# Three kinds of values turned by VectorE and DRAM instead of TensorE in a four-branch hybrid backbone

## The chip, the cores and the metric

One core of a Trainium2 chip runs the whole kernel in one launch. The metric is the device time of one execution in microseconds (us), the median of several.

## What is computed

Two layers of a backbone over 128 context tokens and 512 latent tokens (`T = 640` together), model width 1024, everything in float32. In each layer a modulated RMS norm gives `h`; one projection `h @ w_in` feeds four mixers of width 512: retention, a gated linear recurrence, a gated DeltaNet and HGRN2. Three of them have four heads of width 128 and run in both directions. Their outputs are gated, projected, summed and added to the residual. Cut to the values, the `v` below, which are what the change is about:

```python
(aq, ak, av, az, bx, bz, cq, ck, cv, cz, ca, cb, dq, df, di, dz, mg) = jnp.split(h @ w_in, offs, axis=-1)
# retention: values av.  kv = sum_j k_j k_dec_j v_j ; o = (q k^T * decay) v + q_dec (q state)
o_intra = jnp.einsum('bnhij,bnjhe->bnihe', scores, v)
kv = jnp.einsum('bnjhd,jh,bnjhe->bnhde', k, k_dec, v)
# DeltaNet: values are silu(conv(cv)); scaled by beta, then a triangular solve
rhs_v = jnp.moveaxis(v * beta[..., None], 3, 2)
# HGRN2: values di, used as in retention with a decay of its own for each channel
kv = jnp.einsum('bnjhd,bnjhe->bnhde', k * jnp.exp(bc[:, :, -1:] - bc), v)
```

## The kernel before

`layer_jobs` makes a list of jobs. A job is one weight tile of 128 columns: `load_w` (L332) loads 512 KB on SyncE's (SP's) queue, `split_w` copies it to a high part on ScalarE (`whi`, L359) and subtracts on VectorE for the low part (`wlo`, L361), and `product` (L376) multiplies in three passes (high by high, high by low, low by high) over eight pieces of 128 rows, first for tokens 0 to 383, then for 384 to 639: 48 matmuls a tile. The result lies channel by token, 128 x 640, and is evacuated from PSUM (`pj`, two banks) by a function `ev_*`. Raw tiles, high parts and low parts have two buffers each.

Beside the jobs run the mixers, Python generators in two lanes, G (DeltaNet heads) and HRL (HGRN2, retention and recurrence heads, alternating). After each piece of `product` the function `pace` advances the generator whose time has come by a count of TensorE time (`clock`, the numbers in `yield`). Each lane has one PSUM tile of two banks for wide results (`M2`, L171 and after). A scheduler then sets the final order on each engine; engines and queues run in that order.

A mixer that sums over tokens needs its values token by channel. `transposes` (five 128 x 128 transposes on TensorE, L301, into an `M2` tile) turns them:

- retention: `ret_in` projects `ak`, `aq`, then `av`, evacuated by `ev_copy` on ScalarE (L496). `ret_mix` waits for `av`, transposes it, copies it to `rvt` on ScalarE (L1298), yields 1.5, and goes on with the transposes of the keys. `rvt` is first read by the state matmuls (`m<-rvt,rkt`).
- HGRN2: `hgrn_in` projects `dq`, two `df`, then `di` (L496); `hgrn_mix` waits for `di`, transposes it and copies it to `hvt` (L1136). `hvt` is first read after seven levels of score work.
- DeltaNet: `gdn_prep` convolves `cv` into `vs`, transposes that, and one VectorE instruction (L939) scales it by 0.5 and the key norms `ik` into `vt`, read in `gdn_chain`.

The products of `rest` (modulation of later parts, `mod_dots`, L630, 64 loads and 128 VectorE dot products `mjunk`) run as fill beside the first heads of layer 0. `finish` stores a head's result to DRAM on SP's queue (`br<-fbr`, L565). `gdn_solve` and `gdn_inv` already move blocks of 32 through DRAM (`l_dr`, `d_dr`, loads `dct`, L992), and one VectorE transpose in blocks of 32 stands in L998.

Of the kernel before, what the change touches and what calls it, by code (L numbers as in the profile page):

```python
# [23 lines left out]
F32 = mybir.dt.float32  # L24
F32R = mybir.dt.float32r
U8 = mybir.dt.uint8
AF = mybir.ActivationFunctionType
# [47 lines left out]
def conv_off(t):  # L75
    return 0 if t == 0 else SC + 3 + 128 * (t - 1)
# [3 lines left out]
def hybrid_kernel(ctx: ExitStack, tc: tile.TileContext, I, O):  # L80
# [81 lines left out]
    def t3(ap, n=NT):  # L162
        return ap.rearrange("p (t c) -> p t c", t=n)

    def ts(t):
        return slice(128 * t, 128 * t + 128)
# [355 lines left out]
        return f  # L522


    def transposes(src_of, n=NT):
        ps = M2()
        for t in range(n):
            tr(ps[:, ts(t)], src_of(t), ident)
        return ps
# [244 lines left out]
    def layer(l, hh, hl):  # L774
# [6 lines left out]
        def proj_to(S, key, name, i, evac, shape=None, after=None):  # L781
# [5 lines left out]
                S[key] = x  # L787
            return Job(I['w_in'][l, CIDX[name, i]], run, cost=2 if name == 'df' else 1)

        def zproj(name, i, S):  # L790
            extra_jobs.append(proj_to(S, 'z', name, i, ev_silu2))
            zout[lane[0] - 1] = 1
            extra_jobs[-1].urgent = True
# [77 lines left out]
        def gdn_prep(h, S):  # L871

            yield lambda: 'ck' in S
            cs = gdn_conv(h, S, 'ck')
            yield LV
            ps = transposes(lambda t: cs[:, conv_off(t):conv_off(t) + 128])  # L880
            ss = sum_squares(t3(ps))
            S['kt'] = U(name="kt")
            A.activation(S['kt'], ps, AF.Copy)
            V.tensor_scalar(ss, ss, 4 * EPS, None, op0=OP.add)
            rk, ik = small_tile([128, NT], "rk", 1), small_tile([128, NT], "ik", 1)
            power(ik, ss, phalf)
            V.reciprocal(rk, ss)
            b2, kd = small_tile([128, 2, NT], "b2", 1), small_tile([128, 2, NT], "kd", 1)
            for d in range(2):
                c = 4 * d + h  # L890
                V.tensor_tensor(b2[:, d], rk, gg['beta'][:, :, c], op=OP.mult)
                V.tensor_tensor(kd[:, d], b2[:, d], gg['kd'][:, :, c], op=OP.mult)
            S['b2'], S['kd'] = b2, kd
            yield 2
            gms = []
            for d in range(2):
                R = gc_rows(d, h)
                msk = K('add_f') if d == 0 else K('add_b')
                V.tensor_tensor(t3(R), t3(R), msk[:, None, :].to_broadcast([128, NT, 128]), op=OP.add)
                for t in range(NT):  # L900
                    A.activation(R[:, ts(t)], R[:, ts(t)], AF.Exp, bias=gg['gcn'][:, t, 4 * d + h:4 * d + h + 1])
                gms.append(R)
            kc = S['kn'] = cs

            def tk(t):
                return kc[:, conv_off(t):conv_off(t) + 128]
            ps = M2()
            for t in range(NT):
                mm(ps[:, ts(t)], tk(t), tk(t), start=True, stop=True)
            for d in range(2):  # L910
                at = U(name="at")
                for t in range(NT):
                    V.scalar_tensor_tensor(at[:, ts(t)], ps[:, ts(t)], b2[:, d, t:t + 1],
                                           gms[d][:, ts(t)], op0=OP.mult, op1=OP.mult)
                S['at', d] = at
            yield gdn_solve(h, S)
            yield 2
            yield lambda: 'cq' in S
            qs = S['qn'] = gdn_conv(h, S, 'cq')
            yield LV  # L920
            sq = U([128, PADW], name="sq")
            A.activation(sq[:, :CONVW], qs[:, :CONVW], AF.Square)
            ps = column_sums(lambda t: sq[:, conv_off(t):conv_off(t) + 128])
            S['eps'] = small_tile([128, NT], "ssq", 1)
            V.tensor_scalar(S['eps'], ps, EPS * 128, 4 * EPS * EPS * 128, op0=OP.mult, op1=OP.add)
            yield 2
            ps = M2()
            for t in range(NT):
                mm(ps[:, ts(t)], tk(t), qs[:, conv_off(t):conv_off(t) + 128], start=True, stop=True)
            for d in range(2):  # L930
                V.tensor_tensor(gms[d], ps, gms[d], op=OP.mult)
                S['attn', d] = gms[d]
            yield 1.5
            yield lambda: 'cv' in S
            vs = gdn_conv(h, S, 'cv')
            yield LV
            ps = transposes(lambda t: vs[:, conv_off(t):conv_off(t) + 128])
            S['vt'] = U(name="vt")
            V.scalar_tensor_tensor(t3(S['vt']), t3(ps), 0.5, ik[:, :, None].to_broadcast([128, NT, 128]),  # L939
                                   op0=OP.mult, op1=OP.mult)  # L940
            yield 1

        def gdn_solve(h, S):
# [99 lines left out]

        def gdn_chain(h, S):
            kn, kt, vt = S['kn'], S['kt'], S['vt']
            SH, VN, QE = {}, {}, {}
            for d in range(2):
                SH[d] = U(name="gS")
# [63 lines left out]
        def hgrn_in(h, S):  # L1112
            def gates(d):
                def after(th):
                    c = 8 * l + 4 * d + h
                    k = S['k', d] = UP(name="hk%d" % d)
                    V.tensor_scalar(k, th, hbn[:, c:c + 1], hb[:, c:c + 1], op0=OP.mult, op1=OP.add)
                    V.tensor_scalar(th, th, hb[:, c:c + 1], ha[:, c:c + 1], op0=OP.mult, op1=OP.add)
                    V.tensor_scalar(th, th, 1e-30, None, op0=OP.max)
                return after  # L1120
            return [proj_to(S, 'q', 'dq', h, ev_silu2)] + \
                [proj_to(S, ('f', d), 'df', 4 * d + h, ev_tanh, after=gates(d)) for d in range(2)] + \
                [proj_to(S, 'v', 'di', h, ev_copy)]

        def hgrn_mix(h, S):
            yield lambda: 'v' in S
            q, kf, kb, ff, fb = S['q'], S['k', 0], S['k', 1], S['f', 0], S['f', 1]
            ks = U(name="hks")
            V.tensor_tensor(ks, kf, kb, op=OP.add)
# [1 line left out]
            V.tensor_tensor(cb[:, 0], q, fb, op=OP.mult)  # L1131
            V.tensor_tensor(cb[:, 1], q, ff, op=OP.mult)
            C, B_ = cb[:, 0], cb[:, 1]
            ps = transposes(lambda t: S['v'][:, ts(t)])
            vt = U(name="hvt")
            A.activation(vt, ps, AF.Copy)  # L1136
            free(1)
            yield LH0
            def blocks(w, f):

# [122 lines left out]
        def ret_in(h, S):  # L1263
# [22 lines left out]
            def job(nm, scale):  # L1286
                evac, after = rotated(scale)
                return proj_to(S, nm, nm, h, evac, after=after)
            return [job('ak', 128.0 ** -0.5), job('aq', None), proj_to(S, 'av', 'av', h, ev_copy)]

        def ret_mix(h, S):
            ret_tables(h)
            yield lambda: 'av' in S
            q, k, v = S['aq'], S['ak'], S['av']
            zproj('az', h, S)
            ps = transposes(lambda t: v[:, ts(t)])
            vt = U(name="rvt")
            A.activation(vt, ps, AF.Copy)  # L1298
            free(1)
            yield 1.5  # L1300
            ps = transposes(lambda t: k[:, ts(t)])
            kts = []
            for d in range(2):
# [524 lines left out]
```

## Time and profile before

| | |
|---|---|
| median of 3 runs | 2066.72 us (2066.12 to 2068.05) |
| the profiled execution | 2062.44 us, its span 2060.7 us |
| granted TensorE clock | 0.996 of 2.4 GHz over the span |
| busy share of the span | PE 98%, VectorE 68%, ScalarE 44%, GpSimd 4% |
| DMA | 245 MB, 119 GB/s in the mean |

The span lies 1.7 us under its own execution's time, and that 4.3 us under the median of the runs. A stage is read best as a stretch of the trace: the mixers of layer 0 run from about 60 to 860 us, those of layer 1 from 1060 to 1830, and between and behind them stand products with little beside them.

### The profile page before, as it was taken

To read this page: it belongs to the slowest core of one execution; us is meant where nothing else is said; L and a number is where in the kernel's file an instruction comes from. 1 tells how busy PE (TensorE), PEld (TensorE's weight loads), DVE (VectorE), ACT (ScalarE), POOL (GpSimd) and SP (SyncE) were. 2 spreads that over 40 slices of the span, in tenths; PEclk is the share of its full clock that TensorE was granted. 3 is DMA by queue.
4 is the path that set the end of the run, shared out by engine and by line. 5 is a ranking of instruction groups with operands and counts; after the bars stand their busy time and mean duration, and the time that the engine had idled before them with its cause. 6 is when DMAs were issued, how large, how long until landed. Compare 5 with 4: busy or idle time off the path is not lost.

```text
span 2060.7 us, 42665 instructions
## 1 busy us (share of the span) xinstructions
PE 2021.5 (98%) x17362; PEld 1979.1 (96%) x17362; DVE 1403.5 (68%) x3164; ACT 907.9 (44%) x1940; POOL 75.7 (4%) x195
## 2 busy tenths in 40 slices
PE   7999999999999999999999999999999999999997
PEld 5999999999999999999989999999999999999997
DVE  5799998668757845368578556855784685552775
ACT  4543455455545445322244536444643554362221
POOL 0000000000000000000000000000000000000000
PEclk9999999999999999999999999999999999999999
DMA  8246642323323242465413223232332233243632
GB/s 323 86 125 192 195 159 87 97 84 110 100 79 101 78 123 80 152 213 159 152 55 102 84 84 101 76 104 73 123 93 79 77 111 106 94 154 114 213 128 95
DMA packets 133305, 245.24 MB, mean 119 GB/s; under 512 B 44069, under 2 KB 59125, under 8 KB 132981
## 3 DMA queue, kind: packets, MB, share of 16 engines
q1 hardware_dynamic: 131956, 239.90, 36.0%
q8 instruction: 136, 2.23, 0.5%
q10 hardware_dynamic: 1152, 2.62, 0.3%
q14 instruction: 61, 0.49, 0.1%
HBM read 205.20 MB, written 37.27 MB: 118 GB/s over the span
## 4 chain that ended last, share of the span: by engine, by line
PE 89%; DVE 5%; DMA 3%; ACT 2%; issue 1%; SPq 1%; POOL 0%; DVEq 0%; ACTq 0%
PE pj L376 73%; PE m L297 13%; PE m L301 2%; DVE mjunk L630 1%; PE wide L384 1%; DMA wss<-in_w_ss 1%; DMA R<-gc 1%; DVE wlo L361 1%; DMA dct<-d_dr 0%; DMA sW<-l_dr 0%; DMA par<-in_params 0%; DVE cs L855 0%; ACT dfull L1002 0%; ACT whi L359 0%; DMA wm<-in_w_mod 0%
## 5 line engine op out<-in xcount | busy, mean ns | idle before, releaser
L376 PE MATMUL pj<-hh,whi 128*128 128x256 f32 (+2 forms) x2896 | 912.8, 315 | 2.6 <-ACT mg L521 1.0
L376 PE MATMUL pj<-hl,whi 128*128 128x256 f32 (+2 forms) x2896 | 903.7, 312 | 0.1
L376 PE MATMUL pj<-hh,wlo 128*128 128x256 f32 (+1 forms) x2880 | 897.7, 312 | 0.0
L376 PEld LDWEIGHTS pj<-hh,whi 128*128 128x128 f32 (+1 forms) x2896 | 547.4, 189 | 6.3 <-ACT mg L521 1.6
L376 PEld LDWEIGHTS pj<-hl,whi 128*128 128x128 f32 (+1 forms) x2896 | 547.8, 189 | 2.0 <-DVE hl L104 0.5
L376 PEld LDWEIGHTS pj<-hh,wlo 128*128 128x128 f32 x2880 | 545.4, 189 | 1.2
L361 DVE TENSOR_TENSOR wlo<-wraw,whi 128x1024 fp32r<-128x1024 f32 x228 | 278.7, 1222 | 157.5 <-ACT whi L359 155.4
L359 ACT ACTIVATE whi<-wraw 128x1024 fp32r<-128x1024 f32 x230 | 243.6, 1059 | 321.4 <-PE pj L376 286.4
L376 PE MATMUL pj<-bl,whi 128*128 128x384 f32 (+1 forms) x512 | 158.2, 309 | 0.0
L376 PE MATMUL pj<-bh,whi 128*128 128x384 f32 (+1 forms) x512 | 158.2, 309 | 0.0
L376 PE MATMUL pj<-bh,wlo 128*128 128x384 f32 (+1 forms) x512 | 157.7, 309 | 0.0
L376 PEld LDWEIGHTS pj<-bh,whi 128*128 128x128 f32 x512 | 96.4, 188 | 0.0
L376 PEld LDWEIGHTS pj<-bh,wlo 128*128 128x128 f32 x512 | 96.3, 188 | 0.0
L376 PEld LDWEIGHTS pj<-bl,whi 128*128 128x128 f32 x512 | 96.2, 188 | 0.0
L521 ACT ACTIVATE mg<-pj 128x384 f32<-128x384 f32 (+1 forms) x128 | 54.9, 430 | 85.1 <-PE pj L376 84.6
L630 DVE SCALAR_TENSOR_TENSOR mjunk<-wm,cs 128x512 bf16<-128x512 f32 x128 | 87.8, 686 | 1.5 <-DMA wm<-in_w_mod 0.9
L376 PE MATMUL pj<-yl,whi 128*128 128x256 f32 (+1 forms) x256 | 78.9, 309 | 0.0
L376 PE MATMUL pj<-yh,whi 128*128 128x384 f32 (+1 forms) x256 | 78.6, 309 | 0.0
L376 PE MATMUL pj<-yh,wlo 128*128 128x256 f32 (+1 forms) x256 | 78.0, 309 | 0.0
L543 ACT ACTIVATE junk<-m 128x128 bf16<-128x128 f32 x160 | 44.4, 278 | 68.1 <-PE m L297 56.5
L967 DVE TENSOR_TENSOR sW<-sW,sLt 128x126 f32<-128x126 f32 (+22 forms) x248 | 62.8, 253 | 10.4 <-ACT hkst L1181 2.7
L969 DVE TENSOR_TENSOR sW<-sW 128x126 f32<-128x126 f32 (+22 forms) x248 | 62.6, 252 | 4.7
(394 smaller groups left out, 2898.5 us busy)
## 6 DMA issues: line engine op xcount, KB each, us to landing
wraw<-in_w_in SPq DMA_DIRECT2D x184, 512.0 KB
mg<-mg SPq DMA_DIRECT2D x96, 320.0 KB
wm<-in_w_mod SPq DMA_DIRECT2D x64, 256.0 KB
wraw<-in_w_branch SPq DMA_DIRECT2D x32, 512.0 KB
R<-gc SPq DMA_DIRECT2D x32, 320.0 KB
braw<-br SPq DMA_DIRECT2D x32, 320.0 KB
wss<-in_w_ss SPq DMA_DIRECT2D x32, 256.0 KB
wraw<-in_w_out SPq DMA_DIRECT2D x16, 512.0 KB
```

The lines of the kernel that those rows point to most:

```text
L297: return PE.matmul(out, lhsT, rhs, **k)
L301: return PE.transpose(out, in_, idn)
L359: A.activation(hi, raw, AF.Copy)
L361: behind(lambda: (lo_on or j.lo_on or V).tensor_sub(lo, raw, hi.bitcast(F32)), after)
L376: PE.matmul(ps[:m, :b - a], w[:, k0 + k], r[k][:, a:b], start=(k + n == 0), stop=(k == nk - 1 and n == len(ops) - 1))
L384: PE.matmul(ps[:m, :b - a], w[:, k], r[k][:, a:b], start=(k + n == 0), stop=(k == nk - 1 and n == (2 if lo else 1)))
L521: A.activation(dst[:, a:b], ps, AF.Tanh, scale=0.5)
L543: A.activation(junk, src3[:, t, :], AF.Square, accum_out=ss[:, t:t + 1])
L630: V.scalar_tensor_tensor(junk, w, 1.0, cs[2 * g + a], op0=OP.mult, op1=OP.mult, accum_out=macc[l][:, c, 2 * g + a:2 * g + a + 1])
L967: V.tensor_tensor(tv, X3[:, :m, i:i + 1].to_broadcast([128, m, n]), L3[:, i:i + 1, i + 1:].to_broadcast([128, m, n]), op=OP.mult)
L969: V.tensor_tensor(X3[:, :m, i + 1:], X3[:, :m, i + 1:], tv, op=OP.subtract)
```

## The change

The values are projected as the first job of their head. VectorE evacuates them with a transpose in blocks of 32 x 32 (`ev_turn`), which leaves the blocks in the wrong places; `turned_out` stores the 128 x 640 tile to DRAM, and `turned_in` loads it back with four DMAs, one for each 32 partitions, in pieces of 32 floats (128 bytes), which puts the blocks where they belong. The DeltaNet's values, which pass a convolution first, are turned from SBUF. Their scaling by `ik` moves to the start of `gdn_chain`. The mixers now wait for the last of their other jobs.

```diff
+    def ev_turn(dst):
+
+        def f(ps, a, b):
+            V.transpose(dst[:, a:b], ps)
+        return f
+
+    def turned_out(x):
+
+        d = dr.tile([128, T], F32, tag="turn", name="turn", bufs=6)
+        nc.sync.dma_start(d, x)
+        return d
+
+    def turned_in(dst, d):
+
+        for a in range(4):
+            nc.sync.dma_start(dst[32 * a:32 * a + 32].rearrange("p (t b c) -> p t b c", t=NT, b=4),
+                              bass.AP(tensor=d.tensor, offset=d.offset + 32 * a, ap=[[T, 32], [128, NT], [32 * T, 4], [1, 32]]))
...
+        def proj_turned(S, key, name, i):
+
+            def run(hi, lo):
+                x = UP(name="p_" + name)
+                yield from product(hi, lo, hh, hl, ev_turn(x), halves=halves)
+                S[key] = turned_out(x)
+                free(1)
+            return Job(I['w_in'][l, CIDX[name, i]], run, cost=1)
...
-            ps = transposes(lambda t: vs[:, conv_off(t):conv_off(t) + 128])
-            S['vt'] = U(name="vt")
-            V.scalar_tensor_tensor(t3(S['vt']), t3(ps), 0.5, ik[:, :, None].to_broadcast([128, NT, 128]),
-                                   op0=OP.mult, op1=OP.mult)
+            vx = U(name="vx")
+            for x0, x1, o in ((0, SC, 0), (SC, T, SC + 3)):
+                V.transpose(vx[:, x0:x1], vs[:, o:o + x1 - x0])
+            vd = turned_out(vx)
+            yield 1
+            vt = S['vt'] = U(name="vt")
+            turned_in(vt, vd)
+            S['ik'] = ik
             yield 1
...
         def gdn_chain(h, S):
             kn, kt, vt = S['kn'], S['kt'], S['vt']
+            V.scalar_tensor_tensor(t3(vt), t3(vt), 0.5, S['ik'][:, :, None].to_broadcast([128, NT, 128]),
+                                   op0=OP.mult, op1=OP.mult)
...
-            return [proj_to(S, 'q', 'dq', h, ev_silu2)] + \
-                [proj_to(S, ('f', d), 'df', 4 * d + h, ev_tanh, after=gates(d)) for d in range(2)] + \
-                [proj_to(S, 'v', 'di', h, ev_copy)]
+            return [proj_turned(S, 'v', 'di', h), proj_to(S, 'q', 'dq', h, ev_silu2)] + \
+                [proj_to(S, ('f', d), 'df', 4 * d + h, ev_tanh, after=gates(d)) for d in range(2)]
...
-            yield lambda: 'v' in S
+            yield lambda: ('f', 1) in S
...
-            ps = transposes(lambda t: S['v'][:, ts(t)])
             vt = U(name="hvt")
-            A.activation(vt, ps, AF.Copy)
-            free(1)
+            turned_in(vt, S['v'])
...
-            return [job('ak', 128.0 ** -0.5), job('aq', None), proj_to(S, 'av', 'av', h, ev_copy)]
+            return [proj_turned(S, 'av', 'av', h), job('ak', 128.0 ** -0.5), job('aq', None)]
...
-            yield lambda: 'av' in S
-            q, k, v = S['aq'], S['ak'], S['av']
+            yield lambda: 'aq' in S
+            q, k = S['aq'], S['ak']
             zproj('az', h, S)
-            ps = transposes(lambda t: v[:, ts(t)])
             vt = U(name="rvt")
-            A.activation(vt, ps, AF.Copy)
-            free(1)
-            yield 1.5
+            turned_in(vt, S['av'])
```

What the two programs hold: TensorE 14582 matmuls before, 14462 now (five transposes for each of 24 values less, everything else the same); VectorE 48 transposes more; ScalarE 48 instructions less; SP's queue 120 DMAs more (24 stores, 96 loads).

First place, TensorE, retention of head 0 in layer 0: the row of the values' five transposes between two products. Before:

```order
L376 MATMUL pj<-hh,whi 128x256
L376 MATMUL pj<-hl,whi 128x256
L376 MATMUL pj<-hh,wlo 128x256
L301 MATMUL m_2381<-ident,p_av 128x128 x5
L376 MATMUL pj<-hh,whi 128x384
L376 MATMUL pj<-hl,whi 128x384
L376 MATMUL pj<-hh,wlo 128x384
```

Now the first transposes of that mixer are those of the keys:

```order
L376 MATMUL pj<-hh,whi 128x384
L376 MATMUL pj<-hl,whi 128x384
L376 MATMUL pj<-hh,wlo 128x384
L301 MATMUL m_2393<-ident,p_ak 128x128 x5
L376 MATMUL pj<-hh,whi 128x256
L376 MATMUL pj<-hl,whi 128x256
L376 MATMUL pj<-hh,wlo 128x256
```

The row of `p_av` is gone and no other took its place.

Second place, SP's queue in layer 0, where the first fill loads (`wm`) come. Behind a row stands what it waits for: `DVE` a VectorE instruction, `DMAHW` an earlier DMA's landing. Before:

```order
L332 DMA wraw<-in_w_in 128x1024 [waits DVE_49]
L956 DMA sW<-l_dr 20x1024 [waits DMAHW2_49,DMAHW1_49,DMAHW3_49,DMAHW0_49,Pool_49]
L956 DMA sW<-l_dr 20x1024 [waits DMAHW7_49]
L1435 DMA mg_162<-mg 128x640 [waits Activation_49]
L332 DMA wraw<-in_w_in 128x1024 [waits DVE_49]
L627 DMA wm<-in_w_mod 128x512 [waits DVE_49]
```

Now:

```order
L332 DMA wraw<-in_w_in 128x1024 [waits DMAHW6_49,DMAHW4_49,DVE_49]
L534 DMA turn<-vx 128x640 [waits DMAHW7_49,DVE_49]
L1462 DMA mg_162<-mg 128x640 [waits DMAHW0_49,Activation_49]
L540 DMA vt<-turn 32x20x32 [waits DMAHW7_49,DMAHW1_49]
L540 DMA vt<-turn 32x20x32 [waits DMAHW2_49]
L540 DMA vt<-turn 32x20x32 [waits DMAHW3_49]
L540 DMA vt<-turn 32x20x32
L332 DMA wraw<-in_w_in 128x1024 [waits DVE_49]
L645 DMA wm<-in_w_mod 128x512 [waits DMAHW6_49,DVE_49]
```

The DeltaNet's store waits for the turn on VectorE, its first load back for the store's landing, and weight loads stand behind both. The stores and loads of HGRN2 and retention stand apart from each other in the queue.

Third place, VectorE in layer 0, close to the last of the fill products. Before:

```order
L630 SCALAR_TENSOR_TENSOR mjunk,macc_168<-wm,cs_1772 128x512
L630 SCALAR_TENSOR_TENSOR mjunk,macc_168<-wm,cs_1767 128x512
L563 SCALAR_TENSOR_TENSOR fbr<-m_3199,ghg,p_cz 128x640
L851 TENSOR_SCALAR cs<-p_ck,par 128x644
L1185 COPY_PREDICATED hscb<-lvm,m_3648 128x160
```

Now:

```order
L361 TENSOR_TENSOR wlo<-wraw,whi 128x1024
L648 SCALAR_TENSOR_TENSOR mjunk,macc_168<-wm,cs_1763 128x512
L895 SCALAR_TENSOR_TENSOR cs<-cth,cs 128x644
L528 STREAM_TRANSPOSE p_av<-pj 128x384
L648 SCALAR_TENSOR_TENSOR mjunk,macc_168<-wm,cs_1773 128x512
```

A turn out of PSUM now stands between fill products; from the first to the last of them three values are turned there, and one right ahead of the first.

## Rows read from the trace of the kernel before

**Rows 1.** The page, part 1: busy us, share of the span, instructions.

```profile
PE 2021.5 (98%) x17362; PEld 1979.1 (96%) x17362; DVE 1403.5 (68%) x3164; ACT 907.9 (44%) x1940; POOL 75.7 (4%) x195
```

**Rows 2.** The page, part 4: the chain that ended last, by engine.

```profile
PE 89%; DVE 5%; DMA 3%; ACT 2%; issue 1%; SPq 1%; POOL 0%; DVEq 0%; ACTq 0%
```

**Rows 3.** Stretches: us, busy us by engine, clock, DMA share, GB/s; both mixer stages.

```profile
60.00:860.00 800.00, 796.00 (x7148) 779.15 (x7147) 601.77 (x1471) 386.89 (x877) 35.03 (x83) 1.00 0.37 116
...
1060.00:1830.00 770.00, 765.16 (x6926) 749.07 (x6925) 508.59 (x1142) 373.18 (x837) 32.87 (x83) 1.00 0.29 93
```

**Rows 4.** Line L301, the transposes: ns min/median/max, first and last start us.

```profile
L301 PE MATMUL m<-ident,cs x80: 270/272/332, 61.4 to 1687.2; 128*128 128x128 f32 x80
...
L301 PE MATMUL m<-ident,p_di x40: 271/272/328, 92.3 to 1662.7; 128*128 128x128 f32 x40
...
L301 PE MATMUL m<-ident,p_av x40: 270/272/329, 193.2 to 1750.3; 128*128 128x128 f32 x40
```

**Rows 5.** Timeline of PE about one value's transposes: start us, us.

```profile
193.07 0.28 PE L376 MATMUL pj<-hh,wlo 128*128 128x256 f32 x1
193.19 0.71 PE L301 MATMUL m<-ident,p_av 128*128 128x128 f32 x5
193.65 0.43 PE L376 MATMUL pj<-hh,whi 128*128 128x384 f32 x1
193.91 0.34 PE L376 MATMUL pj<-hl,whi 128*128 128x384 f32 x1
194.09 0.34 PE L376 MATMUL pj<-hh,wlo 128*128 128x384 f32 x1
```

**Rows 6.** ScalarE's copies of values, by tile; and the first reads of `hvt`.

```profile
L496 ACT ACTIVATE p_av<-pj x16: 362/426/493, 148.0 to 1704.7; 128x384 f32<-128x384 f32 x8, 128x256 f32<-128x256 f32 x8
L1298 ACT ACTIVATE rvt<-m x8: 687/695/707, 195.1 to 1750.8; 128x640 f32<-128x640 f32 x8
L297 PE MATMUL m<-hvt,hkt x128: 270/275/377, 159.2 to 1729.4; 128*128 128x128 f32 x128
...
L1136 ACT ACTIVATE hvt<-m x8: 684/700/712, 97.5 to 1663.0; 128x640 f32<-128x640 f32 x8
```

**Rows 7.** VectorE: the transpose in blocks of 32, and the scaling of `vt`.

```profile
L998 DVE STREAM_TRANSPOSE dcn<-dct x16: 334/346/347, 209.2 to 1725.2; 128x160 f32<-128x160 f32 x16
L939 DVE SCALAR_TENSOR_TENSOR vt<-m,ik x8: 817/822/826, 124.5 to 1687.6; 128x640 f32<-128x640 f32 x8
```

**Rows 8.** The stretch of the fill products, columns as in Rows 3, and these products.

```profile
105.00:305.00 200.00, 197.19 (x1799) 191.76 (x1799) 191.61 (x522) 89.82 (x195) 8.31 (x22) 1.00 0.53 167
L630 DVE SCALAR_TENSOR_TENSOR mjunk<-wm,cs x128: 649/685/694, 105.1 to 304.8; 128x512 bf16<-128x512 f32 x128
```

**Rows 9.** Groups by line: the first pass of the products, with PE's idle before it.

```profile
L376 PE MATMUL pj<-hh,whi 128*128 128x256 f32 (+2 forms) x2896 | 912.8, 315 | 2.6 <-ACT mg L521 1.0 <-ACT p_av L496 0.8 <-DVE p_dz L516 0.7
```

**Rows 10.** Timelines of SP and ACT: a weight load, and its split; and both lines' first starts.

```profile
188.27 0.33 SPq L332 DMA_DIRECT2D wraw<-in_w_in  x1
201.47 1.06 ACT L359 ACTIVATE whi<-wraw 128x1024 fp32r<-128x1024 f32 x1 [2.00 <-PE pj L376]
L359 ACT ACTIVATE whi<-wraw x230: 1040/1061/1098, 19.0 to 2032.7; 128x1024 fp32r<-128x1024 f32 x115
L332 SPq DMA_DIRECT2D wraw<-in_w_in x184: 327/328/1659, 13.5 to 1865.9; - x184
```

**Rows 11.** Waits of SP's queue: us in total, times, longest us.

```profile
SPq L565 <- DVE fbr L563: 56.9, 18, 10.4
```

**Rows 12.** Timelines of SP and DVE: 80 KB loaded in 640 pieces; a stretch, as Rows 3.

```profile
1534.13 0.45 SPq L992 DMA_DIRECT2D dct<-d_dr  x1
1536.40 0.34 DVE L998 STREAM_TRANSPOSE dcn<-dct 128x160 f32<-128x160 f32 x1 [1.88 <-DMA dct<-d_dr]
1535.10:1536.00 0.90, 0.90 (x7) 0.90 (x7) 0.00 (x0) 0.66 (x1) 0.00 (x0) 1.00 0.82 160
```

**Rows 13.** Timelines of SP and PE: start of one `ret_mix`, and its first read of `rvt`.

```profile
1560.05 0.42 SPq L1252 DMA_DIRECT2D tab<-in_tables  x1
1577.86 1.05 PE L297 MATMUL m<-rvt,rkt 128*128 128x128 f32 x8
```

## The prediction

> **What bounds the kernel now.** I read the busy shares first. TensorE is busy for 98% of the span, VectorE for 68%, ScalarE for 44% [rows 1]. A busy TensorE can be one that waits inside its instructions, so the chain of waits comes next: 89% of it is TensorE, 5% VectorE, 3% DMA [rows 2]. Then the stretches, to see whether this holds where the change lies. In the mixers of layer 0 TensorE is busy for 796.0 of 800 us, in those of layer 1 for 765.2 of 770, at the full 2.4 GHz in both (clock 1.00), while VectorE is busy for 75% and 66% and DMA for 37% and 29% [rows 3]. So the reader is to see a kernel in which nearly every microsecond of TensorE's work in the mixers is a microsecond of the span, and in which only 4.0 + 4.8 us of waits could still be taken away there. One place is less comfortable: while the fill products run, from 105 to 305 us, VectorE too is busy, for 191.6 of 200 us [rows 8].
>
> **What is removed.** Each of 24 values (eight heads of three kinds, over two layers) loses five transposes: 40 on `p_av`, 40 on `p_di`, and half of the 80 on `cs`, whose other half are keys [rows 4]. One transpose shows 272 ns, but they overlap, so I price the group by starts. A product's matmul of 256 columns follows the one before it after 0.12 us; the five transposes begin at 193.19 and the next product matmul at 193.65, which is 0.46 us; and that matmul takes 0.26 us to its successor's start where 0.18 is usual, another 0.08 to 0.09 [rows 5]. So a value costs 0.55 us, and 24 cost 13.2 us. From below it is 24 x 0.46 = 11.0, if the bubble behind them stays with whatever comes next; from above 24 x 0.71 = 17.0, the groups' own duration [rows 5]. I take 13.2, since the starts show it. A group that the scheduler splits costs about the same: what is paid goes with the number of transposes.
>
> ScalarE loses 32 evacuations of about 0.43 us and 16 copies of 0.70 [rows 6], together 24.9 us. I cost this at nothing: ScalarE is busy for less than half of either mixer stage [rows 3], and it doesn't set the pace.
>
> **What is added on VectorE.** The nearest row is the same instruction, 346 ns for 160 columns [rows 7], or 2.16 ns a column, so 1.38 us for a value's 640 and 33.2 us for 24. From below, a single pass over 640 columns is 0.82 us [rows 7], or 19.7 us. I take 33.2. Over the span VectorE goes from 1403.5 to about 1437 us, some 70%, and most of it lies beside products. The cover is thin only in the stretch of the fill products: four values are turned in it or right ahead of it, 4 x 1.38 = 5.5 us, against 8.4 us in which VectorE is idle there [rows 8]. TensorE may have to wait for some of that, since the low parts of the weights come from the same in-order engine. I take half, 2.7 us, with 0 and 5.5 as ends.
>
> The turned evacuations hold a `pj` bank for up to 384 x 2.16 ns = 0.83 us where ScalarE's copy held it for 0.43. The other bank gives a product 24 matmuls of at least 0.12 us [rows 5], or 2.9 us, so this is hidden as long as VectorE is not over 2 us late. The row that shows such waits has TensorE idle for 2.6 us in all before 2896 matmuls, 0.7 of it for an evacuation that VectorE ends [rows 9]. I cost it at nothing. The scaling of `vt` moves and stays one instruction of 0.82 us; it reads a tile that was loaded long before.
>
> **What is added on SP's queue and the DMA rings.** There are 24 stores and 96 loads, 120 issues of 0.33 to 0.45 us [rows 10, 12], about 48 us of a queue that mostly waits. A quarter of a return is 640 pieces of 128 bytes, as is the load of `dct` in the trace: 2.3 us from its issue to its first use, and the rings busy for 0.82 of 0.9 us meanwhile [rows 12]. So a return costs four issues (1.6), the last quarter's 2.3 and up to three more times 0.74 on the rings, 6.1 us, or 4 x 2.3 = 9.2 if nothing overlaps; the rings are busy for 3.0 us a return, 71 us in all, over 1570 us of mixers in which they are two thirds idle [rows 3].
>
> Who waits for that? HGRN2's values are first read some 60 us after the point where they were copied (97.5 and 159.2 us for the first head) [rows 6]. The DeltaNet's must pass the inverse first. Retention's are closest: from the load of its tables, behind which the return now stands, to the first read are 17.8 us [rows 13], of which I take 4 us off for the removed step. That leaves 13.8 for 6.1 to 9.2 us. I cost it at nothing.
>
> What is queued behind is the other question. A weight load issued at 188.27 is split at 201.47, 13.2 us later, and the first load of the kernel shows that 5.5 us are enough (13.5 to 19.0) [rows 10]. So the queue can be held for 7.7 us before a split comes late. A DeltaNet value holds it longest: the store waits for VectorE, for which the stores of `fbr` are the nearest row, 56.9 us in 18 waits, 3.2 each [rows 11]; then 0.4 to issue, 2.3 to land, 1.6 for the loads: 7.5 us. That just fits. In the others the store and the return stand apart.
>
> **The sum.** The profiled execution took 2062.4 us, 1.7 over its span. 2062.4 - 13.2 + 2.7 = 2051.9. It lies 4.3 us under the median of the runs, which I add: **2056.2, so 2056 us.** A measurement of this kernel can tell 0.2%, about 4.1 us, from no change; the forecast is 0.5%.
>
> **Rivals.** *VectorE takes over (0.15).* The queue on VectorE is in order, and with 191.6 of 200 us it has no reserve in the first heads [rows 8]. It decides from the point where more than the idle 8.4 us come into that stretch, for instance because a mixer that starts earlier brings its own work in. If eight of 24 values end uncovered, 11.0 us come back: 2066.7 - 13.2 + 11.0 = 2064.5, no change. Against it: outside that stretch VectorE is idle for a quarter and more. About half of this case lies on the side of faster.
>
> *SP's queue stops the weights (0.05).* One DeltaNet store that waits as long as the longest `fbr`, 10.4 us [rows 11], holds the queue for 14.7 us, and the split comes 7.0 us late. In eight values that is 56 us: 2066.7 - 13.2 + 56 = 2110, slower. It is slower by 0.2% from (13.2 + 4.1) / 8 = 2.2 us late each, a hold of 9.9 us. Against it: a split stands ahead of its product by some microseconds more, and the scheduler places a store near the time at which it is ready.
>
> *The return is late (0.04).* If small pieces take three times what the rows say, a return is 18.3 us, retention's matmuls wait for 4.5 us in each of eight heads, and the time is 2066.7 - 13.2 + 36 = 2090. The row of `dct` speaks against it: its pattern is the same and it took 2.3 us [rows 12]. The Trainium skill, page "VectorE: DVE Perf Modes", section "The three transpose paths", warns of just this: a plain DMA copy that transposes by strides is 19 times slower than the crossbar's transpose when the innermost stride at the destination is large. Taken as 19 x 2.3 = 44 us a return, an estimate by that page, the sum would be about 2066.7 - 13.2 + 8 x 30 = 2290 us. The trace disagrees for this pattern, as its pieces of 128 bytes are contiguous on both sides.
>
> That the change doesn't do what it says gets no chance: the built program has 120 transposes less on TensorE and no other matmul more.
>
> **How the numbers follow.** The forecast has 0.76, the rivals 0.15, 0.05 and 0.04. Faster by over 0.2%: 0.76 and half of VectorE's case, 0.84. Within: 0.07 of VectorE's case and a weak form of the queue's, 0.08. Slower: the rest, 0.08. The range begins at 2066.7 - 13.2 - 3.0 = 2050.5, with nothing given back and some of the 8.8 us of waits in the mixers gone with the transposes that shared a PSUM tile [rows 3]. Its upper end is 2064, the bounds 11.0 for the gain and 5.5 for VectorE (2061.2) and into VectorE's case; what is left out is under 2 in 10.
>
> **What the changed profile would show.** Right: TensorE busy for about 2008 us, 98% of a span near 2050; no `p_av` or `p_di` in the transposes and half the `cs`; turns of 0.83 us for 384 columns; TensorE's idle before products still a few us; weight splits still waiting for TensorE and not for a load. Wrong: TensorE waiting for `wlo` or a turn between 100 and 330 us (VectorE), a split that waits for `wraw` (SP's queue), or `rvt` matmuls that wait for a DMA (the return). If the turns cost far less than 1.38 us a value, the 2.7 us were too many; if TensorE's work falls by much other than 13 us, the price by starts was wrong.

## The result, and the profile after

The changed kernel took 2078.01 us (median of 5 runs, 2075.0 to 2081.76) against 2066.72: ratio 1.0059, 95% interval 1.0046 to 1.0071. It is 0.6% slower, where 0.5% faster was forecast. The profiled execution took 2081.76 us, its span 2080.0, against 2060.7 before: 19.3 us more. The medians lie 11.3 us apart, so some 8 us of what the two traces show apart is scatter: the execution traced before was faster than its median, the one traced now slower.

The page of the changed kernel, busy time by engine:

```profile
PE 2020.6 (97%) x17242; PEld 1976.7 (95%) x17242; DVE 1416.7 (68%) x3212; ACT 886.5 (43%) x1892; POOL 77.3 (4%) x195
```

120 transposes are gone (x17362 before, x17242 now), yet TensorE is busy for 2020.6 us after 2021.5 [rows 1]. I count a busy microsecond at half clock as half a microsecond of work (matmuls of 384 columns start 0.32 us apart there, 0.17 at full clock), and so split the span of each trace in three: time in which TensorE is idle (span less busy), time that the clock lost (half of all stretches granted at 0.50), and the rest, its work at full clock. Before, the record shows two such stretches, 16.9 us in all (6.8 at 1288 us, 10.1 at the end), in the changed kernel eight, 41.2 us.

| us | span | idle | lost by the clock | work |
|---|---|---|---|---|
| before | 2060.7 | 39.2 | 8.5 | 2013.0 |
| changed | 2080.0 | 59.4 | 20.6 | 2000.0 |
| difference | +19.3 | +20.2 | +12.1 | -13.0 |

Idle time inside a stretch at half clock stands in both columns, and the last such stretch is counted to its own end, which lies up to 2 us behind the span. Counted once and inside the span, the work is 2018.4 and 2006.1 us, 12.3 less. So the transposes did give back what was forecast, 12.3 to 13.0 us for 13.2. Waits and the clock took 32 us in these two traces; by the medians, which differ by 11.3, some 24.

Where? Both mixer stages of the changed kernel; it is 28 us late from the end of the first on, so the stretches end, and the second begins, 28 us later than before (us, busy us by engine, clock, DMA share, GB/s):

```profile
60.00:888.00 828.00, 805.13 (x7111) 787.20 (x7110) 609.15 (x1499) 377.92 (x853) 35.19 (x83) 0.98 0.40 122
1088.00:1858.00 770.00, 764.98 (x6917) 749.02 (x6916) 517.07 (x1166) 362.62 (x816) 34.84 (x83) 1.00 0.34 103
```

In layer 0 TensorE is now idle for 22.9 us where it was for 4.0 [rows 3], at a mean clock of 0.98; in layer 1 for 5.0 after 4.8, at full clock. By the starts of the same matmuls (the first to the 5400th of the products, and on to the 10200th), layer 0 went from 972.0 to 998.5 us and layer 1 from 893.0 to 884.9.

Closer: the stretch from the 600th to the 1800th matmul of the products holds most of the loss, and it holds most of the fill. Before, then changed:

```profile
156.30:387.30 231.00, 228.70 (x2027) 222.87 (x2025) 208.79 (x563) 108.18 (x251) 10.44 (x24) 1.00 0.49 153
```

```profile
157.40:413.70 256.30, 240.08 (x2105) 233.04 (x2104) 226.87 (x607) 109.58 (x250) 11.09 (x24) 0.96 0.49 149
```

It is 25.3 us longer. Idle time went from 2.3 to 16.2 us, the clock took 10.2 more. I call the sum, 2.3 before and 26.4 now, **the stretch's loss**, and use it below: it shows what the median of a whole run hides.

Who is waited for, in TensorE's waits from 150 to 450 us (line and tile waited for; us in all, times, longest; the four largest of nine):

```profile
PE m L297 <- DVE gS L1128: 4.3, 3, 1.9
PE pj L376 <- DVE p_bz L516: 4.1, 3, 2.0
PE pj L376 <- ACT p_cq L508: 3.9, 1, 3.9
PE pj L376 <- DVE p_dz L516: 1.9, 2, 1.4
```

No turn and no weight stands among the nine. They are evacuations and steps of the first DeltaNet head's chain (`gS`, `r`, `gvn`), and the timeline of the longest case shows how they come about (start us, us; rows of other engines and lines left out):

```profile
286.51 0.34 DVE L1128 SCALAR_TENSOR_TENSOR gS<-gS,etot,m 128x128 f32<-128x128 f32 x1
...
287.50 0.69 DVE L648 SCALAR_TENSOR_TENSOR mjunk<-wm,cs 128x512 bf16<-128x512 f32 x1
...
288.12 1.22 DVE L361 TENSOR_TENSOR wlo<-wraw,whi 128x1024 fp32r<-128x1024 f32 x1
...
289.26 0.34 DVE L1128 SCALAR_TENSOR_TENSOR gS<-gS,etot,m 128x128 f32<-128x128 f32 x1
...
289.65 0.49 PE L297 MATMUL m<-gS,cs 128*128 128x128 f32 x2 [1.76 <-DVE gS L1128]
...
297.59 0.28 ACT L561 ACTIVATE junk<-m 128x128 bf16<-128x128 f32 x1 [2.98 <-PE m L297]
...
300.83 0.28 ACT L507 ACTIVATE p_cq<-pj 128x128 f32<-128x128 f32 x1 [0.51 <-DVE lbr L1429]
...
301.44 0.69 PE L376 MATMUL pj<-hh,whi 128*128 128x384 f32 x1 [3.88 <-ACT p_cq L508]
```

A state `gS` of 0.34 us stands in VectorE's queue behind a fill product (0.69) and a split (1.22). TensorE waits 1.76 us for it; what it computes next comes late to ScalarE, which waits 2.98; the evacuation of `p_cq` stands behind that on ScalarE, and the last 0.51 us before it are a wait for VectorE again (`lbr`); TensorE waits another 3.88 for its bank. Three queues in order hand one delay round. The clock's loss then comes on top:

```profile
286.00:300.00 14.00, 8.13 (x49) 7.39 (x48) 13.93 (x36) 9.04 (x21) 1.09 (x1) 0.88 0.50 147
300.00:308.00 8.00, 6.56 (x34) 6.27 (x35) 7.83 (x20) 3.83 (x10) 1.79 (x4) 0.57 0.42 125
```

VectorE is busy for 21.8 of these 22 us. Its own price of the turn, by line:

```profile
L528 DVE STREAM_TRANSPOSE p_av<-pj 128x384 f32<-128x384 f32 (+1 forms) x16 | 8.2, 514 | 2.4 <-PE pj L376 2.2
L528 DVE STREAM_TRANSPOSE p_di<-pj 128x384 f32<-128x384 f32 (+1 forms) x16 | 8.2, 511 | 3.4 <-PE pj L376 3.1
L966 DVE STREAM_TRANSPOSE vx<-cs 128x128 f32<-128x128 f32 (+1 forms) x16 | 7.2, 488 | 0.0
...
L1077 DVE SCALAR_TENSOR_TENSOR vt<-vt,ik 128x640 f32<-128x640 f32 x8 | 6.6, 825 | 7.5 <-DMA vt<-turn 7.5
```

The three turns are 23.6 us for 24 values, 0.98 each; VectorE's busy time over the span rose by 13.2 (1403.5 to 1416.7), as its records overlap in part.

### The profile page after: what moved, and what is told of

Same layout as the page of the kernel before. It is cut to its first block, busy times and chain, and to the rows that moved or that the text cites. A ratio compares the mean times of both kernels' runs of the same rounds, so it can differ in the third digit from the quotient of the medians.

```text
span 2080.0 us, 42678 instructions
## 1 busy us (share of the span) xinstructions
PE 2020.6 (97%) x17242; PEld 1976.7 (95%) x17242; DVE 1416.7 (68%) x3212; ACT 886.5 (43%) x1892; POOL 77.3 (4%) x195
## 3 DMA queue, kind: packets, MB, share of 16 engines
q8 instruction: 135, 2.21, 0.4%
## 4 chain that ended last, share of the span: by engine, by line
PE 54%; DVE 2%; DMA 1%; SPq 1%; ACT 0%; issue 0%; POOL 0%; DVEq 0%; ACTq 0%
PE pj L376 47%; PE m L297 7%; PE m L301 1%; SPq L1012 0%; DMA d_dr<-sW 0%; DMA dct<-d_dr 0%; DMA R<-gc 0%; DVE xn L104 0%; DVE y L104 0%; SPq L540 0%; DMA sW<-l_dr 0%; DVE wlo L361 0%; ACT whi L359 0%; POOL rs L600 0%; DVE cs L882 0%
## 5 line engine op out<-in xcount | busy, mean ns | idle before, releaser
L376 PE MATMUL pj<-hh,whi 128*128 128x256 f32 (+2 forms) x2896 | 914.4, 316 | 17.1 <-DVE p_bz L516 5.5
```

Of the source, the lines that this page charges most:

```text
L376: PE.matmul(ps[:m, :b - a], w[:, k0 + k], r[k][:, a:b], start=(k + n == 0), stop=(k == nk - 1 and n == len(ops) - 1))
```

## The experiments

Theories: **A**, VectorE's time for the turns; **B**, the order (values first) in itself, B2 where it means layer 0 alone; **C**, or **D** when it is about layer 0 alone, the 120 DMAs on SP's queue and the rings; **F**, formed after the first four runs: the fill, pulled forward and packed into VectorE's order, leaves no slack, and any new order then pays in waits. Ratios are to the kernel before, run beside each; the stretch's loss and the work come from one trace of each run, and two traces of the same layer 0 (kernel before and e1) differ by 2.4 us in that loss.

| run | ratio (95%) | stretch's loss, us | work, us |
|---|---|---|---|
| kernel before | 1 | 2.3 | 2013.0 |
| changed kernel | 1.0059 (1.0046 to 1.0071) | 26.4 | 2000.0 |
| e1 layer 1 only | 0.9979 (0.9966 to 0.9992) | 4.7 | 2007.5 |
| e2 order only | 1.0060 (1.0038 to 1.0081) | 11.0 | 2011.9 |
| e3 ScalarE copies | 1.0067 (1.0052 to 1.0082) | 30.0 | 1999.8 |
| e4 fill held | 0.9998 (0.9989 to 1.0008) | 1.3 | 2001.0 |
| e5 turn, values last | 1.0029 (1.0018 to 1.0040) | 8.3 | 2008.4 |
| e6 fill held in layer 0 | 0.9968 (0.9956 to 0.9980) | 1.9 | 1999.7 |
| e7 before, held so | 1.0034 (1.0022 to 1.0045) | 1.7 | 2010.5 |
| e8 DeltaNet only | 0.9979 (0.9969 to 0.9989) | 7.2 | 2008.8 |
| e9 order only, held so | 0.9956 (0.9944 to 0.9968) | 0.5 | 2009.3 |
| e10 HGRN2 first | 1.0002 (0.9989 to 1.0015) | 9.9 | 2011.6 |
| e11 retention first | 1.0009 (1.0000 to 1.0017) | 6.3 | 2015.3 |
| e12 held, spread | 0.9979 (0.9970 to 0.9988) | 7.0 | 2000.8 |
| e13 before, light fill | 1.0067 (1.0055 to 1.0079) | 17.9 | 2015.5 |
| e14 changed, light fill | 1.0015 (1.0003 to 1.0028) | 18.3 | 2001.7 |
| e15 order, light fill | 1.0043 (1.0027 to 1.0060) | 10.0 | 2014.4 |
| e16 compose | **0.9926** (0.9914 to 0.9938) | 1.0 | 2004.3 |
| e17 GpSimd's queue | 1.0303 (1.0282 to 1.0325) | 24.3 | 2001.5 |
| e18 swap | 1.0004 (0.9994 to 1.0013) | 3.9 | 2013.0 |

**Which layer, and is it the order, the turns or the fill (e1 to e4)?**

```diff
 e1    the turned jobs and loads only if l == 1
 e2    return [proj_to(S, 'v', 'di', h, ev_copy), q, f, f]   ('av' likewise; transposes as before)
 e3  -            V.transpose(dst[:, a:b], ps)
     +            A.activation(dst[:, a:b], ps, AF.Copy)       (vx likewise)
 e4  +                edge['lo'] = (...).tensor_sub(lo, raw, hi.bitcast(F32)).ins
     ...
     +                with tc.issue_after(edge['lo']):
                          V.scalar_tensor_tensor(junk, w, 1.0, ...)
```

> Values turned by VectorE and DRAM in layer 1 only; layer 0 is the kernel before, instruction for instruction. Theory A (VectorE's queue: the loss comes where the fill products keep VectorE full, which is in layer 0 alone; TensorE then waits and its clock falls): layer 1 keeps its gain, 6.6 us by the transposes and up to 8.3 by the two traces, so 2058 to 2061. Theory B (projecting the values first puts the order of the mixers out of step, in either layer) and theory C (the 120 DMAs more on SP's queue and the rings are late, in either layer): half of the measured change of +11.3 us, so about 2072.

0.9979, 2059.53 us: theory A's figure in microseconds, and neither B's nor C's, which had it slower. The kernel before took 2064.11 beside it, so the gain is 4.6 us, where A had 5.7 to 8.7. The loss is layer 0's. (Layer 0 is here the kernel before, instruction for instruction, and its stretch's loss is 4.7 against 2.3: so much one execution differs from another.)

> HGRN2's and retention's values are projected first and their mixers wait for the last job, in both layers, but every value is still transposed by TensorE; no turn, no store, no load more. Theory A: VectorE has nothing more to do, so within 4 us of the kernel before, 2063 to 2071. Theory B: the whole loss stays and the transposes are not saved, so 2078 + 13 = 2091. Theory C: as the kernel before, 2067.

1.0060: against theory A and C. Nothing is turned, nothing more is on VectorE or SP's queue, and the time is as much longer as with the whole change. B is right in sign, though it had said 2091 and got 2075.55: the order costs 12 us, and the turns on top of it, with 13 us of work less, gain nothing.

> The changed kernel, with ScalarE copying where VectorE turns (the two evacuations of a value and the copy of the DeltaNet's convolved values); the stores and the loads in pieces stay. Left out is the transpose inside the blocks of 32, so the values used are not the reference's. Theory A: VectorE loses 24 us of work, ScalarE has room for it, the waits in layer 0 go for the most part: 2053 to 2062. Theory B and theory C: nothing that matters to them is touched, 2078 within 4 us.

1.0067, as B and C said. The loss doesn't need VectorE's time for turning: theory A falls.

> The changed kernel, with each modulation dot product tied behind the low part of the weight tile that the program has reached, so that the scheduler cannot pull the fill forward: it spreads over about 70 weight tiles of layer 0 and 20 of layer 1 instead of 22. No work is added or taken away. Theory A: VectorE has slack again where the first heads run, so the waits go and the 13 us of the transposes stay saved: 2050 to 2060. Theory B and theory C: 2078 within 4 us.

0.9998, 2063.22 us: by the ratios 13 us faster than the changed kernel, though short of 2050 to 2060. The stretch's loss is gone (1.3 us); but layer 1, into which the held fill now reaches, takes 896.2 us where the changed kernel takes 884.9. So it is neither A nor B alone. That the order costs where the fill is packed is theory F; e9 tests it.

**Parts of the change, and the fill held in layer 0 (e5 to e8).** Held in layer 0, layer 1's eight weight columns of fill go to the end of layer 0.

```diff
 e5    return [q, f, f, proj_turned(S, 'v', 'di', h)]         ('av' likewise)
 e6, e7  (changed kernel, kernel before)
     +                with tc.issue_after(edge['lo']) if held_fill[0] else ExitStack():
     ...
     +        held_fill[0] = l == 0
 e8    HGRN2 and retention as before, the DeltaNet as changed
```

> All 24 values turned by VectorE and DRAM, but HGRN2's and retention's are projected last, as in the kernel before, and the mixers wait for them. Theory B2 (layer 0 loses by the order, layer 1 gains by the transposes): the turn without the order keeps layer 1's 7 to 8 us and layer 0's 6.6 of transposes, less up to 5 us of turns in the fill stretch: 0.993 to 0.997 of the kernel before. Theory D (in the fill stretch the DMA returns, which stand in SP's queue ahead of the DeltaNet's loads and of the fill's, cost layer 0 some 10 to 15 us whatever the order): 1.000 to 1.004.

1.0029, in D's range. Its trace doesn't close: the work is 2008.4 us, 8 us over what every other kernel without the 120 transposes has. I found no cause for that and draw nothing else from it.

> The changed kernel with the fill held in place in layer 0 alone; layer 1's eight dot products go where the scheduler pulls them, behind layer 0's, at its end. By the stretches of the run before this one, layer 0 then gains 4 us on the kernel before and layer 1 the 8 us that it has in the changed kernel: 0.993 to 0.996 of the kernel before. If the loss in layer 1 of the run with all fill held was not the fill's: 0.999 to 1.001.

> The kernel before with the fill held in layer 0 alone, nothing turned: the control for the last one. If VectorE had cost the kernel before little (2 to 4 us of waits in the fill stretch): 0.997 to 1.001. The difference between this one and the last is then what the turns and the order are worth when VectorE has room: 13 us by the transposes (0.6%).

0.9968, just outside 0.993 to 0.996, and 1.0034. The changed kernel's stretch, which lost 26.4 us, loses 1.9 with the fill held:

```profile
155.70:393.70 238.00, 236.07 (x2170) 230.16 (x2169) 181.34 (x438) 111.00 (x265) 10.21 (x25) 1.00 0.41 120
```

Between the two runs, which differ only in what the change does, lie 13.2 us (2071.31 and 2058.10): the price of the transposes. That they agree is luck in part, as e9 gets more without one value turned. And holding the fill cost the kernel before 7 us, against expectation: the pile of layer 1's fill at the end of layer 0 (the 3600th to the 4200th matmul of the products) lost 9.3 us there and 11.1 in e6, where it was nothing before.

> Only the DeltaNet's values turned, in both layers; the order of all projections is that of the kernel before. Theory B2: a third of the gain with no loss by the order, 0.997 to 0.999. Theory D: the store that waits for VectorE and the four loads behind it hold SP's queue in the fill stretch, half of layer 0's loss: 1.001 to 1.004.

0.9979, as B2 said. So a DeltaNet store that holds SP's queue does no harm to the time as a whole, though the stretch loses 7.2 us here.

**Is the order free where VectorE has room (e9 to e12)?**

```diff
 e9    e2 with the fill held as in e6
 e10, e11  of e2, HGRN2's order alone; retention's alone
 e12 -        EVERY, done = 3, 0 if l else -14
     +        EVERY, done = 2, -14
     +            yield from modulation(1, cs, 16, 24)         (in layer 0, all fill held)
```

> The order alone (HGRN2's and retention's values projected first, all transposed by TensorE), with the fill held in place in layer 0. The kernel before with the fill held so took 1.0034 of the kernel before, the changed kernel held so 0.9968. Theory F (the order costs its 12 us only because the fill is packed around it, so that VectorE has no room): the order is then free, 1.002 to 1.005, and the turn alone is worth about 13 us. Theory B (the order costs by itself): 1.0034 + 0.006 = 1.009.

0.9956, better than either theory, with all 120 transposes in it. Its stretch against the one before, where VectorE was busy for 208.8 of 231 us:

```profile
154.90:387.50 232.60, 232.12 (x2160) 228.33 (x2159) 170.34 (x409) 114.05 (x264) 10.01 (x24) 1.00 0.37 116
```

VectorE has 62 us to spare, TensorE waits for 0.5 us, and the clock stays full. B falls: with the fill held the order costs nothing. But it also shows that "the turn is worth 13 us" holds for work alone: e6 has 9.6 us less work than e9 and is no faster. Most of that goes at the end of layer 0, where e6 lost 11.1 us and e9, with the same fill there, 1.4; why, no run shows.

> Only HGRN2's values projected first; everything transposed by TensorE, fill as the scheduler puts it. If HGRN2's order carries the loss (its last projections, the two gates, bring VectorE six operations right ahead of the mixer, which before had a projection between): 1.004 to 1.007. If it is retention's: 0.999 to 1.002. If either is only one of many orders that fit the packed fill worse: both above 1.002.

> Only retention's values projected first; everything transposed by TensorE. The counterpart of the last one: 0.999 to 1.002 if HGRN2's order carries the loss, 1.004 to 1.007 if retention's does, above 1.002 for both if neither does alone.

1.0002 and 1.0009: neither carries the loss, which none of the three cases had. In the stretch they lose 9.9 and 6.3 us and gain part of it elsewhere. Together (e2) they cost 0.6%; the parts don't add.

> The changed kernel with all 128 dot products held in place over layer 0, one column of weights behind every second weight tile instead of every third, layer 1's included, so that none are left to pile up at the end of layer 0 (where the run held in layer 0 waited 7.7 us and lost 3.4 by the clock). If that pile-up is what it lost: 2064.5 x 0.9968 - 7 to 11 = 2047 to 2051, 0.991 to 0.994. If the denser fill takes VectorE's room again: 0.997 to 1.002.

0.9979, neither range: the end of layer 0 is cured (0.8 us), but the denser fill costs 7.0 us in the stretch.

**Less fill on VectorE, and the two layers put together (e13 to e16).**

```diff
 e13, e14, e15  (kernel before, changed kernel, e2)
     -                V.scalar_tensor_tensor(junk, w, 1.0, cs[2 * g + a], ...)
     +                V.scalar_tensor_tensor(junk[:, :8], w[:, :8], 1.0, cs[2 * g + a][:, :8], ...)
 e16   layer 0 as e9, layer 1 as the changed kernel
```

> The kernel before with each of the 128 dot products over 8 columns instead of 512; left out is the rest of the modulation sums, so the outputs are not the reference's. Loads and the count of instructions stay. It is the base for the next two. Theory F (VectorE's packing makes the loss): its own waits in that stretch are small, so 0.996 to 1.000 of the kernel before.

> The changed kernel with the same cut, which leaves out the same sums. Theory F: without the packing the 13 us of the transposes show, 0.989 to 0.995 of the kernel before and 10 to 15 us under the last run. Theory B (the order or the DMA returns cost by themselves): 6 to 15 us above the last run, as with the full fill.

> The order alone, all values transposed by TensorE, with the same cut, which leaves out the same sums. Theory F: within 4 us of the kernel before with the cut. Theory B: 12 us above it.

1.0067, 1.0015 and 1.0043 (2078.80, 2069.01, 2072.97 us): none lies where F had it. The three turn round, as F said, the changed kernel being now 9.8 us faster than the base where 10 to 15 were expected, and the order 5.8 faster where within 4 was. But the base is spoiled: with less fill the kernel before got slower by 0.67%. The scheduler pulled the cheap products into 12 weight tiles, where they were in 22, and VectorE's waits from 150 to 255 us in e13 say what stopped it:

```profile
DVE mjunk L630 <- DMA wm<-in_w_mod: 27.5, 24, 3.4
```

It was 0.9 us before (105 to 335 us). VectorE is less busy and still late, because what stands at the head of its queue waits for a load. So less work on VectorE was not enough here: its queue now waited for loads instead. As a proof of F the three runs are inconclusive.

> Layer 0 as in the run with the order alone and the fill held (values first, transposed by TensorE); layer 1 as in the changed kernel (values first, turned by VectorE and DRAM). If the layers add: that run's 0.9956, and 3 to 4 us less by layer 1 (its stretches were 6.8 to 8.2 us under the kernel before in the changed kernels, 4.3 in that run), so 0.993 to 0.995. If the order of one layer upsets the next one's schedule: 0.996 or more.

0.9926, 2049.34 us (2048.97 to 2051.66), 17 us faster than the kernel before and, by the ratios, 27 than the changed one: the layers add, slightly better than expected. Its stretch loses 1.0 us:

```profile
156.60:390.30 233.70, 232.67 (x2161) 228.26 (x2160) 170.38 (x409) 114.17 (x264) 10.00 (x24) 1.00 0.37 115
```

**SP's queue, and an order that has nothing to do with values (e17, e18).**

```diff
 e17 -        nc.sync.dma_start(d, x)
     +        nc.gpsimd.dma_start(d, x)                         (and the four loads)
 e18 -            return [job('ak', 128.0 ** -0.5), job('aq', None), proj_to(...)]
     +            return [job('aq', None), job('ak', 128.0 ** -0.5), proj_to(...)]
```

> The changed kernel with the 24 stores and 96 loads of the turn issued on GpSimd's queue, so that SP's queue is as short as before. Theory D (weights, fill and the DeltaNet's loads are late behind the turn's DMAs on SP's queue): the stretch falls from 26 us of waits and lost clock to the order's own 11, so 0.997 to 1.001 of the kernel before. If SP's queue is not what counts (the rings, or the order alone): within 4 us of the changed kernel, 1.004 to 1.008.

1.0303, outside both ranges. The stretch loses 24.3 us without a single turn on SP's queue, so it is not that queue that makes the loss, unless GpSimd's brings the same by another way. The rest is a wait of its own: VectorE, in order, waits for `vt` (waits of VectorE: us, times, longest), 49.6 us where the changed kernel has 7.5.

```profile
DVE vt L1077 <- DMA vt<-turn: 49.6, 8, 7.2
```

> The kernel before with retention's first two projections exchanged (the queries ahead of the keys); no instruction more or less, nothing turned, the fill pulled forward as before. If any order but the one of the kernel before makes the packed stretch wait: 1.002 to 1.006, with 6 us or more of waits and lost clock in the stretch. If it takes an order that moves work closer to a mixer's start: within 0.1%.

1.0004: not every other order costs, as the second case had it. That an order must change what stands next to a mixer's start to cost anything is argued from this one run; e10 and e11, which do change it, lost 9.9 and 6.3 us in the stretch (3.9 here) and nothing in the whole.

## Why the prediction was wrong

- **The gain was right.** 0.55 us a value by starts, 13.2 in all; the work fell by 13.0 (12.3 counted once), and by 13.2, 12.0, 13.3 and 12.2 in e3, e4, e6 and e12.
- **VectorE's price was too high, and didn't matter.** 1.38 us a value were taken, 0.98 measured, inside the stated ends of 19.7 and 33.2 us. With the turns on ScalarE (e3) the time stayed.
- **The step that failed: "I take half, 2.7", the price of the thin cover.** It was bounded by the work that VectorE gets in the fill stretch (0 to 5.5 us), as if an in-order engine with 191.6 of 200 us busy [rows 8] gave back only what is put into it. The stretch lost 24 us more, the whole trace 32.3 more (some 24 by the medians). The amount of turning did not set it: with the turns on ScalarE the stretch lost 30.0 (e3), with no turn at all 11.0 (e2), with all turns and the fill held 1.9 (e6). The signs named for being wrong hardly came: TensorE waited for no `wlo`, no turn and no `rvt`, and the splits waited for `wraw` 5.1 us in all (1.5 before). The rival that VectorE takes over had the place right and the same wrong price ("eight of 24 values end uncovered").
- **The edit that was never priced: "values are projected first".** The prediction has no term for it, though the change begins with it and it moves the starts of 16 mixers; only the first rival mentions a mixer that starts earlier. Alone it costs 12 us (e2). It is free where the fill is held (e9).
- **The `pj` banks were costed at nothing, "hidden as long as VectorE is not over 2 us late".** For the turned evacuations that came true: TensorE waited for none. But its idle time before the first pass of the products, the row from which the term was read, went from 2.6 us [rows 9] to 17.1, most of it for evacuations of other projections that came late on VectorE and ScalarE:

```profile
L376 PE MATMUL pj<-hh,whi 128*128 128x256 f32 (+2 forms) x2896 | 914.4, 316 | 17.1 <-DVE p_bz L516 5.5 <-ACT p_cq L508 3.9 <-ACT p_df L521 2.2
```

- **The clock was left out.** The sum took waits at their own length; here 20.2 us more of idle time came with 12.1 more lost at 1.2 GHz.
- **What was costed at nothing and was nothing:** ScalarE's relief (21.4 us less, no gain); weight tiles, for which no product waited; SP's issues, though a load took 0.64 us instead of the 0.40 worked out.
- **The return was in time for TensorE, not for VectorE.** TensorE waited for no turned value. But the scaling of `vt` doesn't read "a tile that was loaded long before": VectorE waited for it in seven of eight heads, 7.5 us in all and up to 2.3, of which 0.57 in the stretch, too little for its loss. In e17, whose queue records landings, a quarter landed 2.7 us after its issue (median), which is near the 2.3 taken from `dct`. The Trainium skill, page "VectorE: DVE Perf Modes", section "The three transpose paths", has a plain copy that transposes by strides 19 times slower than the crossbar's transpose when the innermost stride at the destination is large. The prediction put that factor on the 2.3 us of a plain load; no run here has a crossbar's transpose to set it against, and the 44 us worked out from it did not come.
- **Layer 1 did what was forecast:** 8.1 us less where 6.6 of transposes went. Not all of it need be theirs: a wait of 2.63 us for `hvt` at 1285.8 and the clock's 3.4 behind it went too.

Shown is that the loss needs the packed fill (e4, e6) and that the order alone is enough for a loss as large in the time (e2). Not settled: why the changed kernel's stretch loses 26 us and the order's alone 11. VectorE's turning is not it (e3: 30.0), and SP's queue hardly (e17: 24.3); the two programs differ in the order on every engine, and no run here holds that fixed.

## What to carry to other kernels

Price a change of order as a change of its own, and first look where an in-order engine is packed: here the loss was not the work added but waits for short steps that now stood behind something else, 1.6 times as long with the clock. Where a scheduler pulls fill forward, tie the fill down before judging another edit, and do the same to the kernel before, as it isn't free (+0.3% there, e7); here that turned +0.6% into -0.3%, and with the turns kept to layer 1 into -0.7%. Split the span of both traces into work, idle time and clock: it tells in one line whether a forecast gain failed to come or was given back.

## What the runs showed of the hardware

- TensorE's granted clock fell to 1.2 GHz for 3.4 or 6.8 us at a time in the changed kernel's mixers: at 221.5 us behind a wait of 2.01, for 3.4; at 259.0 behind two waits of 1.12 in sum, for 3.4; at 300.0 in a wait of 3.88, for 6.8. A wait of 2.21 us at 1128.2 brought none, so the length of a wait alone did not tell. With half of such a stretch lost, the 1.12 us of waits at 256 cost 2.8.
- A transpose in blocks of 32 cost less for each column the longer it was: 345 ns for 160 columns from SBUF (2.2 a column), 580 for 384 from PSUM (1.5), 672 for 512 from SBUF (1.3).
- A store on GpSimd's queue took that engine 0.6 us and a load 0.77, and moving 120 of them there made the kernel 2.4% slower than with SP's queue.
